# Copies of value sums and of transposed probabilities put ahead on ScalarE, the heads' norm as one power of a sum, three buffers zeroed by ScalarE

## The chip, the cores and the metric

The kernel runs on one core of a Trainium2 chip. The metric is the device time of one execution in microseconds (us), lower is better. Three runs of the kernel before took 1310.02, 1311.20 and 1311.35 us; the median is 1311.2 us. One more execution was taken with the hardware profiler on, and everything that is read from a trace below comes from it.

## The reference, cut to what matters

One step of a decoder layer with 512 prompt tokens and 32 sample tokens (8 sequences of 4), model width 1024. Three mixers work side by side (two convolutions and a 4-head mLSTM), then follow a cross attention over 256 memory tokens and a SwiGLU. The parts that the change touches are the keys and values of the memory, the norm of the mLSTM heads, and the softmax of the cross attention:

```
def memory_kv(mem, g, w_kv):
    kv = rmsnorm(mem, g) @ w_kv
    k, v = jnp.split(kv, 2, axis=-1)
...
        h = num / jnp.maximum(jnp.abs(den), floor)[..., None]
...
    hc = hc * lax.rsqrt(jnp.mean(hc * hc, axis=-1, keepdims=True) + EPS)
...
    pr = jax.nn.softmax(s, axis=-1).astype(h.dtype)
    out = jnp.einsum('bhtm,bmhd->bthd', pr, mv.astype(h.dtype)).reshape(B, T, HX * DX)
```

The sample tokens bring their own memory (32 key blocks and 32 value blocks of 256 KB, streamed from HBM) and their own mLSTM state.

## The kernel before, in words

**Tiling.** Activations stand transposed: channels on the 128 partitions, the 544 tokens along the free axis. Each float32 operand is split into a high and a low float32r part: ScalarE copies the high part, VectorE subtracts it from the source for the low part (`split`, lines 112 to 118). A product is three passes, high with high, high with low, low with high. Each 128-wide output block (`block`, line 291) has 48 matmuls of 272 columns. Its weights come as one 512 KB load into a raw buffer `wr` (4 of them) and are split into a buffer `w` (3 of them).

**Order.** TensorE's instructions run in the order in which the program emits them. Small steps are woven into a block through lists of tokens (`first_o`, `head_1`, `heads`, `after_heads` from line 922, `xside` and `xoside` from line 1341). For the other engines a planner chooses the order ahead of time: among the instructions that are ready by its own count it takes the one with the lowest number. The number is the place in the program, less 150 inside `evacuate`, less 300 for weight loads and their splits, less 600 inside `urgent`. Once planned, each engine, and each DMA queue, works through its list in that order; the head of a list that waits holds up all that is behind it.

**Memory values.** `mem_v` (line 526) multiplies the memory with a quarter of the value weights, in two halves; after the second half two sums [128, 256] stand in two of the four PSUM buffers `s1`. Two copies (line 539) scale them by `rm` and write them into `f1` buffers (ten in all), and from there go two DMAs each. In the first lists the order is: sum of squares for the memory norm (`C`, `mem_cols`), second half of quarter 0, first half of quarter 1, `R` (`mem_rows`: two transposes into another `s1` buffer), second half of quarter 1, the first key block, `t` (`token_cols`), and so on. At the same time ScalarE and VectorE work out the gates of the mLSTM (lines 621 to 670). Counted through the program, the first two copies of `mem_v` have the numbers 584 and 599, the ScalarE instructions of lines 655 to 670 the numbers 451 to 461.

**Heads' norm.** `finish` (line 886) adds the sample part of a head's numerator, squares it on ScalarE with a sum, takes the denominator and the norm through eight small [128, 5] instructions (seven on VectorE, one power on GpSimd), and scales the numerator by the result in five instructions (line 904). `head_out` (line 906) transposes it. For heads 0 to 2 this is emitted inside `evacuate`, for the last inside `urgent`.

**Cross attention.** Three buffers [128, 2, 576] (`mqx` and two of `pm`) are set to zero by GpSimd (lines 1190 to 1194); only their diagonal blocks are written later. `xs_t` (token `T`) transposes a half of the probabilities into one PSUM buffer and splits its two halves; `xs_pv` (token `V`) multiplies them with the values; `t` does the same for the sample tokens; `xs_kv` (token `K`) loads the keys and values of the next head back from HBM and splits them. In the list of block 3 stands `... a07 T01 T00 K1`, in that of block 4 `t0 - V0 ...`. The tokens `t` and `o` are emitted inside `evacuate`.

Of the kernel before, what the change touches and what calls it, by code (L numbers as in the profile page):

```python
# [11 lines left out]
AF = mybir.ActivationFunctionType  # L12
# [3 lines left out]
P = 128  # L16
D = 1024
NP = 512
NS = 32
# [5 lines left out]
NM = 256  # L25
EPS = 1e-6
# [9 lines left out]
def layer(ctx: ExitStack, tc: tile.TileContext, a):  # L36
    nc = tc.nc
# [23 lines left out]
    def pht(shape, dt=F32, tag=None, bufs=1):  # L61
        n = nm(tag or "ph")
        return ph["sb"].tile(shape, dt, tag=tag or n, name=n, bufs=bufs)
# [8 lines left out]
    def pair():  # L72
        return act_t([P, 2, T])

    def f1(shape=None, dt=F32):
        return sb.tile(shape or [P, T], dt, tag="f1", name=nm("f1"), bufs=10)

    def lt(shape=None, dt=F32):
        return sb.tile(shape or [P, T], dt, tag="lt", name=nm("lt"), bufs=8)

    def small(shape, dt=F32, tag="small", bufs=16, ZP=0):
        return (ph["sb"] if ZP else sb).tile(shape, dt, tag=tag, name=nm(tag), bufs=bufs)

    def const(shape, dt=F32):
        n = nm("const")
        return sb.tile(shape, dt, tag=n, name=n, bufs=1)
# [4 lines left out]
    def s1(shape):  # L91
        return ph["ps"].tile(shape, F32, tag="s1", name=nm("s1"), bufs=ph["s1"])

    def TTo(out, x, y, op):
        nc.vector.tensor_tensor(out=out, in0=x, in1=y, op=op)  # L95

    def TS(out, x, s1_, op0, s2=None, op1=None):
        if op1 is None:
            nc.vector.tensor_scalar(out=out, in0=x, scalar1=s1_, scalar2=None, op0=op0)
        else:  # L100
            nc.vector.tensor_scalar(out=out, in0=x, scalar1=s1_, scalar2=s2, op0=op0, op1=op1)

    def STT(out, x, s, y, op0, op1):
        nc.vector.scalar_tensor_tensor(out=out, in0=x, scalar=s, in1=y, op0=op0, op1=op1)  # L104

    def ACT(out, x, f, **kw):
        nc.scalar.activation(out, x, f, **kw)  # L107

    def MM(out, l, r, start, stop):
        nc.tensor.matmul(out, lhsT=l, rhs=r, start=start, stop=stop)  # L110
# [9 lines left out]
    def MS(ap, v):  # L120
        nc.gpsimd.memset(ap.bitcast(F32) if ap.dtype == F32R else ap, v)

    MULT, ADD, SUB, MAX, MIN = ALU.mult, ALU.add, ALU.subtract, ALU.max, ALU.min
# [11 lines left out]
    ones32 = const([P, P])  # L135
# [10 lines left out]
    for h in range(NH):  # L146
        for base in (20, 28, 36, 44):
            for d in range(2):
                order += [("in", base + 2 * h + d)]
                if base == 44 and h == 0 or h == 1 and base < 36:  # L150
                    n = (1, 7)[d] if h == 0 else 2
# [114 lines left out]
    def wget(*key):  # L266
        i = order.index(key)
        assert i == wpos[0] or key in wt, (key, order[wpos[0]])
        while wpos[0] <= min(i + ahead[0], len(order) - 1):
            w_emit(order[wpos[0]])  # L270
            wpos[0] += 1
        return wt.pop(key)
# [18 lines left out]
    def block(key, acts, nbg=0, inner=()):  # L291

        w = wget(*key)
        ps = mm_ps()
        nk, done = len(acts), 0
        for k in range(nk):
            mm_k(ps, w, acts, k, k == 0, k == nk - 1)
            while done < len(inner) and (done + 1) * nk <= (k + 1) * len(inner):
                if inner[done]:
                    inner[done]()  # L300
                done += 1
        background(nbg)
        return ps

    def evacuate(f):

        with tc.high_priority(EVAC):
            f()
# [175 lines left out]
    def part(f, *x):  # L484
        return lambda: f(*x)
# [4 lines left out]
    memg, mst = [], {}  # L490
# [32 lines left out]
    def mem_k(k, hl):  # L523
        return memg[k // 2][:, hl, k % 2, :]

    def mem_v(g, half):

        w = wget("v", g, half)
        if half == 0:
            mst["ps"] = [s1([P, NM]) for _ in range(2)]  # L530
        for mb in range(2):
            ps = mst["ps"][mb]
            for k in range(4 * half, 4 * half + 4):
                for n, (wi, ai) in enumerate(PASSES):
                    MM(ps, mem_k(k, ai)[:, mb * P:(mb + 1) * P], w[:, wi, (k % 4) * NM:(k % 4 + 1) * NM],
                       k == 0 and n == 0, k == 7 and n == 2)
            if half:
                vo = f1([P, NM])
                ACT(vo, ps, AF.Copy, scale=mst["rm"][:, mb:mb + 1])
                nc.sync.dma_start(out=a["pv"][:, mb, g * NM:(g + 1) * NM], in_=vo)  # L540
                nc.sync.dma_start(out=vscr[:, mb, g * NM:(g + 1) * NM], in_=vo)

# [70 lines left out]
    for k in range(8):  # L613
        STT(xr[k], xr[k], col(V_MIX, k), rx, MULT, MULT)
        p = pair()
# [229 lines left out]
    def numer(h, j):  # L845

        if j == 0:
            num = st[h]["num"] = pht([P, 5, E1], tag="num")
            ssq = st[h]["ssq"] = pht([P, 5], tag="ssq", bufs=2)
            MS(num[:, 4, :], 1.0)  # L850
            MS(ssq, 1.0)
        num, ssq, sp, vt = (st[h][x] for x in ("num", "ssq", "sp", "vt"))
        np_ = s1([P, E1])
        for i in range(j + 1):
            for x, (vi, si) in enumerate(PASSES):
                MM(np_, sp[i][:, si, (j - i) * P:(j - i + 1) * P], vt[i][:, vi, :], i == 0 and x == 0,
                   i == j and x == 2)
        ACT(num[:, j, :], np_, AF.Copy)
        ACT(np_[:, :NM], np_[:, :NM], AF.Square, accum_out=ssq[:, j:j + 1])

    def sample(h, b):

# [23 lines left out]
    def finish(h):  # L886

        num, ssq, nps = (st[h][x] for x in ("num", "ssq", "nps"))
        n2 = pht([NS, E1], tag="n2")
        ACT(n2, nps[32:64, :], AF.Copy)  # L890
        TTo(num[:NS, 4, :], nps[0:32, :], n2, ADD)
        ACT(n2[:, :NM], num[:NS, 4, :NM], AF.Square, accum_out=ssq[:NS, 4:5])
        dd, xx, rs = small([P, 5]), small([P, 5]), small([P, 5])
        STT(dd, num[:, :, NM], -1.0, num[:, :, NM], MULT, MAX)
        TTo(dd, dd, tcol[:, :, 64 + h], MAX)
        nc.vector.reciprocal(dd, dd)
        TTo(xx, ssq, dd, MULT)
        TTo(xx, xx, dd, MULT)
        TS(xx, xx, 1.0 / NM, MULT, EPS, ADD)
        nc.gpsimd.tensor_tensor(out=rs, in0=xx, in1=nhalf, op=ALU.pow)  # L900
        TTo(rs, rs, dd, MULT)
        for j in range(5):
            n = P if j < 4 else NS
            TS(num[:n, j, :NM], num[:n, j, :NM], rs[:n, j:j + 1], MULT)

    def head_out(h, d):
# [47 lines left out]
        7: "- - - o0 - o1",  # L954
    }
    before_ops = {"n": numer, "p": sample, "k": k_tok, "c": c_state, "o": head_out}
    head_ops = {"B": m_bcast, "S": scores, "s": scores_s, "V": v_tok}
    other_ops = {"I": mem_in, "t": token_cols, "C": lambda: urgent(mem_cols), "R": lambda: urgent(mem_rows)}

    def side(h, toks):  # L960
        r = []
        for t in toks.split():
            k, x = t[0], [int(y) for y in t[1:]]
            if k == "-":
                r.append(None)
            elif k == "M":
                r += mem_next(1)
            elif k == "P":
                r.append(part(sample, h, 0))
            elif k == "f":  # L970
                r.append(lambda: (urgent if h == NH else evacuate)(lambda: finish(h - 1)))
            elif k in before_ops:
                r.append(part(before_ops[k], h - 1, *x))
            elif k in head_ops:
                r.append(part(head_ops[k], h, *x))
            else:
                r.append(other_ops[k])
        return r
# [80 lines left out]
    for j in range(8):  # L1059
        p = pair()  # L1060
# [6 lines left out]
    for c in range(4):  # L1067
# [23 lines left out]
        p = pair()  # L1091
# [73 lines left out]
    for k in range(8):  # L1165
        x = lt()
# [21 lines left out]


    mqx = pht([P, 2, 576], F32R)  # L1190
    MS(mqx, 0.0)
    pm = [pht([P, 2, 576], F32R) for _ in range(2)]
    for x in pm:
        MS(x, 0.0)
    at = [None] * 8
    xs = [dict() for _ in range(4)]

# [164 lines left out]

    def xrun(t):
        f = part(xops[t[0]], *map(int, t[1:]))
        return (lambda: evacuate(f)) if t[0] in "to" else f

    def xlist(x):
        return [None if t == "-" else xrun(t) for t in x.split()]
# [5 lines left out]
    for j in range(2, 8):  # L1374

        ps = block(("xq", j), xg, inner=xlist(xside[j]))
# [7 lines left out]
    for j in range(8):  # L1384

        ps = block(("xo", j, 0), at[0:4], inner=xlist(xoside[j]))
# [342 lines left out]
```

## Time and profile before

| | |
|---|---|
| median of the runs shown | 1311.2 us (1310.02 to 1311.35) |
| the profiled execution's own time | 1310.46 us |
| its span, first to last instruction | 1308.5 us |
| TensorE matmuls busy | 1287.4 us, 98% |
| VectorE busy | 887.1 us, 68% |
| ScalarE busy | 592.8 us, 45% |
| GpSimd busy | 41.6 us, 3% |
| mean granted TensorE clock | 0.996 of full speed |

The profile gives for each instruction its start and length, and for each idle stretch the instruction whose semaphore ended it. Positions are microseconds from the first instruction. Instructions of one kind that follow each other on an engine are drawn together in a timeline line; "x4" is then their number and the length is that of all together. "L110" is the line of the helper that issues a matmul, L107 that of every ScalarE activation, L95 a VectorE operation on two tensors, L104 one with a scalar and two tensors, L99 and L101 one with scalars only, L121 a GpSimd fill. Between "[" and "]" stands how long the engine was idle before, and what it waited for.

### The profile page before, as it was taken

What the parts mean: (1) busy time and instruction counts of PE and PEld (TensorE: products, weight loads), DVE (VectorE), ACT (ScalarE), POOL (GpSimd) and SP (SyncE); (2) the same over time, 40 slices, a digit from 0 to 9 for tenths busy, and PEclk for the clock granted to TensorE, in tenths of its full rate; (3) what the DMA queues carried; (4) which work ended last, traced back from release to release, by engine and by line L of the source; (5) the groups of instructions that cost most, each with busy time, mean ns of one, the idle gap of its engine ahead of it and who ended that gap; (6) DMA issues with size and microseconds to landing.
All of it is one profiled execution on the core that took longest, in us unless ns stands there. A gap on an engine that the chain in (4) does not pass through costs nothing.

```text
span 1308.5 us, 24803 instructions
## 1 busy us (share of the span) xinstructions
PE 1287.4 (98%) x10164; PEld 1271.9 (97%) x10164; DVE 887.1 (68%) x1486; ACT 592.8 (45%) x1046; POOL 41.6 (3%) x117
## 2 busy tenths in 40 slices
PE   9989999999999999999999999999999999999997
PEld 9989999999999999999999999999999999999997
DVE  6965665655497859976434557886787667777746
ACT  6845545554433222226333446765544444444433
POOL 1000010110010000000000000000000000000000
PEclk9999999999999999999999999999999999999998
DMA  7365644434465233423244224664323233333212
GB/s 262 101 179 172 193 132 137 126 109 148 117 148 168 84 95 82 82 73 89 84 129 147 82 89 144 210 193 142 94 74 113 86 94 109 94 94 94 80 41 69
DMA packets 83265, 155.68 MB, mean 119 GB/s; under 512 B 25124, under 2 KB 33700, under 8 KB 83152
## 3 DMA queue, kind: packets, MB, share of 16 engines
q1 hardware_dynamic: 83152, 154.10, 40.1%
q8 instruction: 80, 1.31, 0.4%
q14 instruction: 33, 0.27, 0.1%
HBM read 137.54 MB, written 16.52 MB: 118 GB/s over the span
## 4 chain that ended last, share of the span: by engine, by line
PE 90%; issue 5%; DVE 2%; ACT 1%; DMA 1%; POOL 0%; SPq 0%; POOLq 0%; DVEq 0%; ACTq 0%
PE mm L110 62%; PE s L110 14%; PE sy L1477 8%; PE sz L1477 4%; PE sx L1477 2%; DVE f L95 0%; ACT w L107 0%; DVE w L95 0%; DMA f<-kscr 0%; ACT act L107 0%; PE s L911 0%; POOL small L381 0%; PE s L827 0%; DMA lt<-in_xT 0%; ACT f L107 0%
## 5 line engine op out<-in xcount | busy, mean ns | idle before, releaser
L110 PE MATMUL mm<-act,w 128*128 128x272 f32 x6336 | 838.0, 289 | 1.9 <-ACT f L107 0.9
L110 PEld LDWEIGHTS mm<-act,w 128*128 128x128 f32 x6336 | 809.7, 189 | 5.1 <-ACT f L107 1.1
L107 ACT ACTIVATE w<-wr 128x1024 fp32r<-128x1024 f32 (+2 forms) x202 | 196.6, 975 | 393.9 <-PE mm L110 229.2
L95 DVE TENSOR_TENSOR w<-wr,w 128x1024 fp32r<-128x1024 f32 (+2 forms) x202 | 225.4, 1116 | 142.7 <-ACT w L107 142.0
L104 DVE SCALAR_TENSOR_TENSOR f<-act,const,f 128x512 f32<-128x512 f32 (+1 forms) x136 | 96.4, 718 | 2.4
L95 DVE TENSOR_TENSOR lt<-mm,lt 128x544 f32<-128x544 f32 x56 | 40.4, 721 | 55.8 <-PE mm L110 55.6
L110 PE MATMUL mm<-act,fw 128*128 128x272 f32 x576 | 76.2, 288 | 0.0
L110 PEld LDWEIGHTS mm<-act,fw 128*128 128x128 f32 x576 | 73.9, 188 | 0.0
L107 ACT ACTIVATE act<-f 128x544 fp32r<-128x544 f32 (+3 forms) x75 | 44.3, 600 | 46.2 <-DVE f L95 40.8
L110 PE MATMUL s<-act,act 128*128 128x256 f32 (+4 forms) x408 | 62.9, 302 | 1.1 <-DVE act L95 0.8
L95 DVE TENSOR_TENSOR act<-f,act 128x544 fp32r<-128x544 f32 (+3 forms) x75 | 48.4, 652 | 20.6 <-ACT act L107 20.3
L95 DVE TENSOR_TENSOR f<-f,f 128x544 f32<-128x544 f32 (+4 forms) x78 | 51.2, 659 | 14.0 <-ACT f L107 12.7
L110 PEld LDWEIGHTS s<-act,act 128*128 128x128 f32 (+1 forms) x408 | 55.0, 184 | 4.2 <-DVE act L95 1.2
L1477 PE MATMUL sy<-bt,w 128*128 128x272 f32 x408 | 56.9, 288 | 0.6 <-ACT f L107 0.6
L1477 PEld LDWEIGHTS sy<-bt,w 128*128 128x128 f32 x408 | 53.3, 188 | 0.8 <-ACT f L107 0.8
L104 DVE SCALAR_TENSOR_TENSOR ct<-ct,wbc,s 128x258 f32<-128x258 f32 x64 | 28.7, 478 | 26.4 <-PE s L110 26.4
L107 ACT ACTIVATE f<-sy 128x272 f32<-128x272 f32 x51 | 19.7, 389 | 39.2 <-PE sy L1477 39.0
L95 DVE TENSOR_TENSOR wr<-wr,wr 128x1024 f32<-128x1024 f32 (+1 forms) x34 | 32.4, 954 | 5.9 <-DMA wr<-in_w_fi 5.5
L95 DVE TENSOR_TENSOR f<-mm,f 128x544 f32<-128x544 f32 (+1 forms) x29 | 20.7, 720 | 22.6 <-PE mm L110 20.4
L107 ACT ACTIVATE fw<-fr 128x512 fp32r<-128x512 f32 x26 | 16.4, 632 | 42.9 <-PE mm L110 41.6
L107 ACT ACTIVATE f<-mm 128x544 f32<-128x544 f32 (+1 forms) x50 | 30.5, 611 | 6.1 <-PE mm L110 5.9
L95 DVE TENSOR_TENSOR xpair<-kr,xpair 128x512 fp32r<-128x512 f32 x46 | 30.5, 681 | 3.5 <-ACT xpair L107 3.4
(237 smaller groups left out, 1405.5 us busy)
## 6 DMA issues: line engine op xcount, KB each, us to landing
wr<-in_w_in SPq DMA_DIRECT2D x74, 512.0 KB, 3.7
wr<-in_w_fi SPq DMA_DIRECT2D x44, 512.0 KB, 3.6
ct<-in_ctn SPq DMA_DIRECT2D x32, 258.0 KB, 3.0
out_sct<-ct SPq DMA_DIRECT2D x32, 258.0 KB, 3.3
kr<-in_ktc SPq DMA_DIRECT2D x32, 256.0 KB, 3.8
kr<-in_vc SPq DMA_DIRECT2D x32, 256.0 KB, 3.9
fr<-in_w_ffn_out SPq DMA_DIRECT2D x32, 256.0 KB, 2.7
lt<-in_xT SPq DMA_DIRECT2D x16, 272.0 KB, 3.7
```

What stands on the lines that cost most here:

```text
L95: nc.vector.tensor_tensor(out=out, in0=x, in1=y, op=op)
L104: nc.vector.scalar_tensor_tensor(out=out, in0=x, scalar=s, in1=y, op0=op0, op1=op1)
L107: nc.scalar.activation(out, x, f, **kw)
L110: nc.tensor.matmul(out, lhsT=l, rhs=r, start=start, stop=stop)
L1477: nc.tensor.matmul(ps, lhsT=w[:, wi, c + k * P:c + (k + 1) * P], rhs=x(k, ai), start=first and k == 0 and n == 0, stop=k == 3 and n == 2, ...
```

## The change

The copies of the value sums in `mem_v` go inside `evacuate`, and so do the steps of token `T`. The squares of the numerator are scaled by 1/16 before they are squared, so that the sum is the mean over 256. With d the greater of |den| and the floor, `finish` no longer divides: the factor (mean(num²)/d² + eps)^(-1/2) / d is written as (mean(num²) + eps·d²)^(-1/2). Three buffers are zeroed by ScalarE copies with the scale 0 in place of GpSimd fills.

```
             if half:
                 vo = f1([P, NM])
-                ACT(vo, ps, AF.Copy, scale=mst["rm"][:, mb:mb + 1])
+                evacuate(lambda: ACT(vo, ps, AF.Copy, scale=mst["rm"][:, mb:mb + 1]))
...
-        ACT(np_[:, :NM], np_[:, :NM], AF.Square, accum_out=ssq[:, j:j + 1])
+        ACT(np_[:, :NM], np_[:, :NM], AF.Square, scale=1.0 / 16, accum_out=ssq[:, j:j + 1])
...
-        ACT(n2[:, :NM], num[:NS, 4, :NM], AF.Square, accum_out=ssq[:NS, 4:5])
+        ACT(n2[:, :NM], num[:NS, 4, :NM], AF.Square, scale=1.0 / 16, accum_out=ssq[:NS, 4:5])
+
         dd, xx, rs = small([P, 5]), small([P, 5]), small([P, 5])
         STT(dd, num[:, :, NM], -1.0, num[:, :, NM], MULT, MAX)
         TTo(dd, dd, tcol[:, :, 64 + h], MAX)
-        nc.vector.reciprocal(dd, dd)
-        TTo(xx, ssq, dd, MULT)
-        TTo(xx, xx, dd, MULT)
-        TS(xx, xx, 1.0 / NM, MULT, EPS, ADD)
+        STT(xx, dd, EPS, dd, MULT, MULT)
+        STT(xx, xx, 1e-37, ssq, MAX, ADD)
         nc.gpsimd.tensor_tensor(out=rs, in0=xx, in1=nhalf, op=ALU.pow)
-        TTo(rs, rs, dd, MULT)
...
     mqx = pht([P, 2, 576], F32R)
-    MS(mqx, 0.0)
     pm = [pht([P, 2, 576], F32R) for _ in range(2)]
-    for x in pm:
-        MS(x, 0.0)
+    for x in (mqx, *pm):
+        ACT(x.rearrange("p a (n c) -> p (a n) c", c=64), ones32[:, 0:64].rearrange("p (o c) -> p o c", o=1)
+            .to_broadcast([P, 18, 64]), AF.Copy, scale=0.0)
...
     def xrun(t):
         f = part(xops[t[0]], *map(int, t[1:]))
-        return (lambda: evacuate(f)) if t[0] in "to" else f
+        return (lambda: evacuate(f)) if t[0] in "toT" else f
```

## Rows read from the trace of the kernel before

**Rows 1.** The first page of the profile: the busy times, with their share of the span, and the shares of the engines in the chain of work that ended last.

```profile
PE 1287.4 (98%) x10164; PEld 1271.9 (97%) x10164; DVE 887.1 (68%) x1486; ACT 592.8 (45%) x1046; POOL 41.6 (3%) x117
PE 90%; issue 5%; DVE 2%; ACT 1%; DMA 1%; POOL 0%; SPq 0%; POOLq 0%; DVEq 0%; ACTq 0%
```

**Rows 2.** The waits of TensorE over the whole span: who waited for whom, us in total, how often, the longest. The two longest are shown.

```profile
PE s L388 <- ACT f L107: 4.7, 1, 4.7
PE s L911 <- DVE num L99: 1.6, 1, 1.6
```

**Rows 3.** The timeline of TensorE from 64 to 84 us: start, length, line, operation.

```profile
64.67 5.92 PE L110 MATMUL s<-w,act 128*128 128x256 f32 x48
70.42 0.91 PE L110 MATMUL mm<-act,w 128*128 128x272 f32 x6
76.02 0.43 PE L388 MATMUL s<-const,const 128*128 128x128 f32 x2 [4.69 <-ACT f L107]
76.21 4.60 PE L110 MATMUL s<-w,act 128*128 128x256 f32 x24
80.65 3.04 PE L110 MATMUL s<-act,w 128*128 128x256 f32 x24
```

**Rows 4.** Busy times by stretch: start and end, length, busy us (instructions) of TensorE, weight loads, VectorE, ScalarE, GpSimd, then the granted TensorE clock, the busy share of the DMA engines and GB/s.

```profile
76.50:79.90 3.40, 3.40 (x18) 3.40 (x17) 0.00 (x0) 0.85 (x2) 0.00 (x0) 0.50 0.80 174
396.20:399.60 3.40, 3.40 (x27) 3.19 (x27) 1.51 (x2) 0.50 (x1) 0.00 (x0) 1.00 0.67 197
```

**Rows 5.** The timeline of ScalarE from 67 to 77 us. "f<-s,const" are the copies of the value sums, "w<-wr" high parts of weights, the rest the gates and, last, the copy of `mem_rows`.

```profile
67.75 1.06 ACT L107 ACTIVATE w<-wr 128x1024 fp32r<-128x1024 f32 x1 [2.23 <-PE s L110]
70.74 0.66 ACT L107 ACTIVATE ph<-f 4x544 fp32r<-4x544 f32 x1 [1.93 <-DVE f L648]
71.47 1.28 ACT L107 ACT_TABLE_LOAD   x1
72.76 0.65 ACT L107 ACTIVATE f<-f 4x544 f32<-4x544 f32 x1
73.44 1.06 ACT L107 ACTIVATE w<-wr 128x1024 fp32r<-128x1024 f32 x1
75.52 0.45 ACT L107 ACTIVATE f<-s,const 128x256 f32<-128x256 f32 x1
76.00 0.45 ACT L107 ACTIVATE f<-s,const 128x256 f32<-128x256 f32 x1
```

**Rows 6.** The timeline of VectorE in the same stretch: the copy of `rm`, the second scan of the gates, and the low parts of two weights.

```profile
66.43 0.49 DVE L515 COPY const<-small 128x2 f32<-128x2 f32 x1 [0.60 <-POOL small L381]
69.36 1.28 DVE L648 TENSOR_TENSOR_SCAN f<-f,f 4x544 f32<-4x544 f32 x1
71.32 1.21 DVE L95 TENSOR_TENSOR w<-wr,w 128x1024 fp32r<-128x1024 f32 x1
74.53 1.23 DVE L95 TENSOR_TENSOR w<-wr,w 128x1024 fp32r<-128x1024 f32 x1 [0.83 <-ACT w L107]
```

**Rows 7.** The timeline of all engines from 383 to 399 us, the last head's `finish`, the fills of the three buffers, and the first transposes of that head.

```profile
386.77 0.40 ACT L107 ACTIVATE n<-num 32x256 f32<-32x256 f32 x1
387.51 0.18 DVE L896 RECIPROCAL small<-small 128x5 f32<-128x5 f32 x1
390.06 1.66 POOL L900 TENSOR_TENSOR small<-small,const 128x5 f32<-128x5 f32 x1 [13.70 <-DVE small L101]
391.68 3.05 POOL L121 MEMSET ph<- 128x1152 f32 x3
395.02 1.02 PE L911 MATMUL s<-const,num 128*128 128x128 f32 x4 [1.64 <-DVE num L99]
397.77 0.60 PE L911 MATMUL s<-const,num 128*128 128x128 f32 x4
```

**Rows 8.** The five scalings of the numerator (L99), as a group: ns shortest, median, longest. The first line is the group from 392 to 396 us (last head), the second that from 180 to 182 us (first head).

```profile
L99 DVE TENSOR_SCALAR num<-num,small x5: 335/342/2383, 392.5 to 395.6; 128x256 f32<-128x256 f32 x4, 32x256 f32<-32x256 f32 x1
L99 DVE TENSOR_SCALAR num<-num,small x5: 336/350/354, 180.6 to 181.7; 128x256 f32<-128x256 f32 x4, 32x256 f32<-32x256 f32 x1
```

**Rows 9.** The timeline of ScalarE after the last head: the weight split at 411 us, and the idle time before it.

```profile
411.08 1.06 ACT L107 ACTIVATE w<-wr 128x1024 fp32r<-128x1024 f32 x1 [3.55 <-issue]
```

**Rows 10.** The timeline around the first `V` token. "act<-s" are parts of the transposed probabilities, "act<-f" the split of the next head's keys, L99 and L1300 the end of the sample's softmax and its transposes (`t0`).

```profile
795.22 0.34 DVE L99 TENSOR_SCALAR f<-f,small 32x256 f32<-32x256 f32 x1
795.49 0.74 DVE L95 TENSOR_TENSOR act<-s,act 128x256 fp32r<-128x256 f32 x2
796.05 0.31 PE L1300 MATMUL s<-const,f 32*128 32x32 f32 x2
797.02 0.63 ACT L107 ACTIVATE act<-f 128x512 fp32r<-128x512 f32 x1 [1.49 <-DMA f<-kscr]
797.89 0.86 PE L110 MATMUL s<-act,act 128*128 128x512 f32 x3
798.58 0.37 ACT L107 ACTIVATE act<-s 128x256 fp32r<-128x256 f32 x1
799.01 0.50 PE L110 MATMUL s<-act,act 128*128 128x512 f32 x1 [0.25 <-ACT act L107]
800.35 2.12 PE L110 MATMUL s<-act,act 128*128 128x512 f32 x8 [0.84 <-DVE act L95]
```

**Rows 11.** DMA issues: KB each, median us from issue to landing.

```profile
vscr<-f SPq DMA_DIRECT2D x8, 128.0 KB, 3.2
```

## The prediction, on record before the changed kernel ran

> **What bounds the kernel now.** I read the first page, then the waits of TensorE, then the timeline around each long wait. On the page the reader sees TensorE busy for 1287.4 us, 98% of the span, and in the chain that ended last 90% TensorE [rows 1]: VectorE and ScalarE have room, so an instruction less on them is worth only what TensorE waits for it. The list of waits then tells where: one of 4.7 us on a ScalarE result and one of 1.6 us on the scaling of a head's numerator [rows 2]. With two short ones of 0.25 and 0.84 us at the first `V` token [rows 10] these lie at the four places that the change touches, so each part is worked out from its own place.
>
> **1. The copies of the value sums.** TensorE reaches `R` at 71.33 us (six matmuls from 70.42 take 0.91) and stands until 76.02: four PSUM buffers hold the two finished sums of quarter 0 and the two half sums of quarter 1, and `R` needs one of them back [rows 3]. The sums ended near 67.6 us (half of the 48 matmuls from 64.67), `rm` was there at 66.92 [rows 6], but the copies start at 75.52 and 76.00 [rows 5], and TensorE goes on 0.05 us after the first ends. In front of them stand gate instructions and a table load; ScalarE even idles 1.93 us before 70.74, so something else held the copies as well. I take it to be their f1 buffer: the second scan of the gates, 69.36 to 70.64, is what sets two of the ten free [rows 6]. From 584 and 599 the change makes 434 and 449, below the gates' 451 to 461. So the copies go right behind the weight split that ends at 68.81, or at worst when the scan is through: 70.64 plus 0.45 is 71.1, before TensorE needs the buffer. Nothing on ScalarE but the gates is behind them, and these move by at most 0.9 us.
>
> The wait costs more than itself. After it the granted clock was 0.50 of full speed, 1.2 GHz, from 76.5 to 79.9 [rows 4], and the next 24 matmuls took 4.60 us where the following 24 took 3.04 [rows 3]: 1.6 us more. After the idle 1.64 us before 395.02 the clock stayed at 1.00 [rows 4, 7]. The whole is 4.69 + 1.6 = 6.3 us.
>
> Late next are the weights. The second half of quarter 1 needs the low part that VectorE makes from 71.32 to 72.53 [rows 6]: TensorE, at that matmul by 71.85, waits 0.7 to 0.8 us. It is through near 75.4. The first key block needs the low part that was made from 74.53 to 75.76 after a high part at 73.44 [rows 5, 6]; with the copies ahead that is up to 0.9 us later, so up to 76.6 against 75.65: 0 to 0.95 us. I take 0.8 + 0.9: the gain is 6.3 - 1.7 = 4.6 us. Bounds: 6.3 if both parts come early, 0 if the copies stay where they are. The three later pairs of copies ended no wait in the list of TensorE, and are put at nothing; their cover is the run of matmuls after them, and without it each would cost its 0.45 us.
>
> **2. The fills and the last head.** TensorE is at the transposes at 393.38 and gets the first scaled part at 395.02 [rows 7]. That scaling took 2.383 us where the median is 0.34 [rows 8]: it began at 392.5 and ended as the three fills on GpSimd ended (391.68 + 3.05 = 394.73). The four after it took 0.34 each, the five of the first head, with no fill beside them, 0.35. With the fills off GpSimd it would end near 392.85, before TensorE asks. So the wait of 1.64 us goes with the fills alone, and the four transposes, spaced by the scalings (1.02 us against 0.60 for the next four [rows 7]), give 0.42 more: 2.05 us.
>
> The Trainium skill ("SBUF — State Buffer", Who interferes with whom) has VectorE and GpSimd share one pair of ports as an exclusive lock in VectorE's 2-port modes, which `tensor_scalar` can enter; the other fully blocks. By it the whole 2.04 us of the long scaling go when the fills go; without it that scaling might have waited for something that stays, and the part would be worth only what the shorter chain gives. The trace agrees with it: a scaling that lasts until the last fill ends.
>
> The shorter chain is then cover only. Between the square (ends 387.2) and the power (390.06) stood four small instructions, so 0.7 us for each with what lies between them; now one, so the power, which ended at 391.72, ends near 389.6, and the first scaling, with the 0.8 us that lay between the two, near 390.8 [rows 7, 8]: 2.6 us before TensorE. The factor 1/16 rides in an instruction that is there. The earlier heads' norms end no wait of TensorE either; nothing is taken for them.
>
> The zeros on ScalarE are not in the trace. From 1.06 us for 1024 columns and 0.66 for 544 [rows 5], 1152 columns make some 1.17 us, three 3.5 us (an estimate). Their place in the list is the planner's. If it is after the last head, the idle 3.55 us before 411.08 [rows 9] hides them. If all three come ahead of the last square, the first scaling moves from 390.8 to 394.3, and 0.9 us of the wait stay. A gain of their own I exclude, since TensorE waits for none. I take nothing, by the idle row; the end 0.9 stays in the range.
>
> **3. Transposed probabilities.** The last quarter of the first head's split starts at 798.58 on ScalarE. Ahead of it stands, besides others, the split of the next head's keys, which waits 1.49 us for its DMA. `V` stops twice, 0.25 and 0.84 us idle [rows 10]; its twelve matmuls, which at the pace of the last eight (2.12 us) take 3.2 us, last from 797.89 to 802.47: 1.4 us lost. Both halves of a transposed tile lie in one PSUM buffer, and the low part of the other half ends at 796.23: if the last high part has to wait for that, it starts at 796.3 and is still in time for 797.89, unless it is again behind the key split. Against it: the sample's softmax now stands behind such splits of 0.37 us, two of them 0.7 us; it ended at 795.56, and its transposes `t0` ran at 796.05, 0.5 us later [rows 10]: up to 0.3 us would be waited there, 0.5 with a low part ahead too. Ends: +1.4 and, if the key split stays ahead and `t0` is late, -0.5. I take 0.9, the one less the other, for all four heads, as the other three show no wait to win.
>
> **The sum.** 4.6 + 2.05 + 0.9 = 7.55 us. Against the profiled execution's 1310.46 us that is 1302.9; this lies 0.74 below the median of the runs shown, so I add half of that: 1303.3 us.
>
> **Rivals.**
> (a) The wait moves to the weights: ScalarE's list puts the key block's high part last, behind all the gates [rows 5]: these end at 75.52, less its own 1.06, plus the copies' 0.9; with 1.06 and VectorE's 1.23 the low part is done at 77.7, TensorE idles 2.0 us instead of 0.9 and falls to 1.2 GHz again (1.6 us). For it: the gates and a table load of 1.28 us stand in the same list. Against it: the weight has the lower number. Then part 1 gives 6.3 - 0.8 - 2.0 - 1.6 = 1.9, the sum is 4.85 and the time 1306.0.
> (b) The change doesn't do what it says: the copies are not ready in the planner's count until the gates are done, and stay. For it: ScalarE idled before 70.74 and they were not taken. Against it: the scan frees buffers in time, and 434 is below 451. Then parts 2 and 3 are left: 1310.46 - 2.95 = 1307.5, and with part 3 at nothing 1308.4 (1309.1 from the median).
> (c) Slower. The copies hold f1 buffers until two DMAs have landed, 3.2 us in the median for the second [rows 11]. If they take them from the gates, the scan waits for a write, then the weight part behind it on VectorE; TensorE waits at quarter 1 as long as it did at `R` (6.3, no gain), and the exponentials of `m_bcast`, four f1 buffers more, wait for the writes of the next pair: two landings and a fall of the clock, 2 x 3.2 + 1.6 = 8.0. Then 1310.46 + 8.0 - 2.95 = 1315.5. It decides from the point where that second wait is over 2.95 us. For it: ten buffers, all in use at the scan. Against it: the copies come ready late in the planner's order, when the gates hold theirs already.
>
> **How the numbers follow.** Forecast 0.62, (a) 0.14, (b) 0.16, (c) 0.08. All terms in full (6.3 + 2.05 + 1.4) give 1300.7; the forecast's own range is 1300.5 to 1305.5. To leave out no more than 2 in 10 the range goes up to (b), 1309.0. About 0.2%, 2.6 us, is what a measurement can tell: faster is below 1308.6. The forecast, (a) and over half of (b) are faster, 0.85; the rest of (b), and (c) where its second wait is short, the same, 0.09; slower 0.06.
>
> **What would show it.** The timeline after: the copies before 71.5 us, `R` without a wait, the clock at 1.00 between 71 and 80, waits under 1 us at the next 48 matmuls (part 1, and (a) if one is longer than 2 us); the last head's five scalings at 0.35 us and no wait at its transposes (part 2); the twelve matmuls of the first `V` without a gap, and whether `t0` waits (part 3). The prediction is wrong if the first copy still starts after 72 us, if a scaling is long without a fill, or if TensorE shows a wait of over 3 us that is not in the list before.

## The result and the profile after

The changed kernel took 1304.3 us in the median of three runs, the kernel before, run beside it, 1311.0 us. The ratio of the means is 0.9947 with a 95% interval of 0.9928 to 0.9967: 6.9 us faster, by the interval 4.3 to 9.4. (A fourth run of the changed kernel was disturbed and took 4426 us; all figures here leave it out.) The forecast was 1303.3 us and faster. The execution whose trace is read below took 1301.8 us, 8.6 us less than the profiled one of the kernel before.

The first page of the profile after, the lines that answer to [rows 1]:

```profile
PE 1284.5 (99%) x10164; PEld 1269.8 (98%) x10164; DVE 883.9 (68%) x1474; ACT 596.2 (46%) x1049; POOL 38.3 (3%) x114
PE 89%; issue 4%; DVE 3%; DMA 2%; ACT 1%; POOL 0%; POOLq 0%; DVEq 0%; ACTq 0%
```

The instruction counts show the norm and the fills: 12 fewer on VectorE (three for each of four heads), three more on ScalarE and three fewer on GpSimd (the fills). The share of TensorE hardly moves, so the waits have to tell where the time went. The waits of TensorE over the whole span, as in [rows 2]:

```profile
PE s L110 <- DVE f L95: 1.5, 1, 1.5
...
PE mm L110 <- DVE lt L104: 1.0, 1, 1.0
...
PE s L110 <- DVE w L95: 0.9, 2, 0.7
...
PE s L1298 <- DVE f L99: 0.2, 1, 0.2
```

The two waits at the top of [rows 2], 4.7 and 1.6 us, are gone; the longest left, 1.5 us, stands in both kernels, far from the change. The other three lines shown are new: the two weights of part 1 (0.9 together), the sample's transposes `t0` of part 3 (0.2), and one of 1.0 us that the prediction did not have, a matmul of a block of the output weights that waits for `lt`.

TensorE's 10164 matmuls stand in the same order in both traces, so the time can be followed by comparing the start of the same matmul (us). The last column is what the change had won up to there, with the 1.09 us that lie ahead of all its parts:

| matmul | before | after | shift so far |
|---|---|---|---|
| six matmuls ahead of `R` | 70.42 | 69.33 | -1.09 |
| `R` | 76.02 | 70.11 | -5.91 |
| last matmul ahead of the last head's transposes | 393.10 | 387.12 | -5.98 |
| first transposes | 395.02 | 387.24 | -7.78 |
| second transposes | 397.77 | 389.56 | -8.21 |
| the matmul that waits for `lt` after the change | 404.73 | 397.56 | -7.17 |
| `t0` of the first head | 796.05 | 789.17 | -6.88 |
| first matmul behind the first `V` | 802.30 | 793.75 | -8.55 |
| end of the span | 1308.5 | 1299.9 | -8.6 |

**Part 1.** The timeline of all engines from 65 to 76 us, against [rows 3, 5, 6] (start, length, engine, line, operation, and in brackets the idle time ahead of it and what ended it):

```profile
68.27 1.28 DVE L648 TENSOR_TENSOR_SCAN f<-f,f 4x544 f32<-4x544 f32 x1
...
69.33 0.91 PE L110 MATMUL mm<-act,w 128*128 128x272 f32 x6
...
69.58 0.84 ACT L107 ACTIVATE f<-s,const 128x256 f32<-128x256 f32 x2 [1.87 <-DVE f L648]
...
70.11 0.43 PE L388 MATMUL s<-const,const 128*128 128x128 f32 x2
70.22 1.21 DVE L95 TENSOR_TENSOR w<-wr,w 128x1024 fp32r<-128x1024 f32 x1
...
71.48 2.89 PE L110 MATMUL s<-w,act 128*128 128x256 f32 x22 [0.70 <-DVE w L95]
...
72.41 1.06 ACT L107 ACTIVATE w<-wr 128x1024 fp32r<-128x1024 f32 x1
...
73.50 1.23 DVE L95 TENSOR_TENSOR w<-wr,w 128x1024 fp32r<-128x1024 f32 x1 [1.74 <-ACT w L107]
...
74.63 0.66 ACT L107 ACTIVATE ph<-f 4x544 fp32r<-4x544 f32 x1
...
74.78 1.93 PE L110 MATMUL s<-act,w 128*128 128x256 f32 x14 [0.17 <-DVE w L95]
```

The copies start at 69.58, in the moment at which the second scan of the gates ends (68.27 + 1.28 = 69.55): nothing but the f1 buffer ties a copy to that scan, so it was the buffer that they had to wait for. `R` follows its six matmuls without a wait. Then come the two weights, 0.70 and 0.17 us. The clock in the same stretch of time as in the first of [rows 4], and over the work behind `R`:

```profile
76.50:79.90 3.40, 3.40 (x32) 3.40 (x32) 2.65 (x3) 1.75 (x3) 0.00 (x0) 1.00 0.78 256
71.50:80.00 8.50, 8.33 (x69) 8.13 (x70) 5.07 (x11) 6.66 (x13) 0.00 (x0) 1.00 0.85 234
```

It is 1.00 throughout: 2.4 GHz where [rows 4] has 0.50. The 22 matmuls behind the weight wait take 2.89 us, where the 24 of that half took 4.60 in [rows 3].

**Part 2.** The last head's scalings as a group, as in [rows 8], and the timeline around them and the next block:

```profile
L99 DVE TENSOR_SCALAR num<-num,small x5: 336/347/354, 383.3 to 384.4; 128x256 f32<-128x256 f32 x4, 32x256 f32<-32x256 f32 x1
```

```profile
381.64 1.67 POOL L899 TENSOR_TENSOR small<-small,const 128x5 f32<-128x5 f32 x1 [11.27 <-DVE small L104]
...
387.24 0.60 PE L909 MATMUL s<-const,num 128*128 128x128 f32 x4
...
391.26 0.63 ACT L107 ACTIVATE k<-kr 128x512 fp32r<-128x512 f32 x1 [6.77 <-DMA kr<-in_ktc]
391.92 0.69 DVE L95 TENSOR_TENSOR k<-kr,k 128x512 fp32r<-128x512 f32 x1 [3.94 <-ACT k L107]
...
393.20 0.90 DVE L104 SCALAR_TENSOR_TENSOR lt<-s,const,lt 128x512 f32<-128x512 f32 x2
...
395.65 2.20 ACT L107 ACTIVATE ph<-const 128x1152 fp32r<-128x1152 f32 x2
...
397.17 0.24 DVE L104 SCALAR_TENSOR_TENSOR lt<-s,const,lt 128x32 f32<-128x32 f32 x1
...
397.56 2.62 PE L110 MATMUL mm<-act,w 128*128 128x272 f32 x19 [0.99 <-DVE lt L104]
```

No scaling is long, and they begin at 383.3, 3.9 us before TensorE asks. Then something is given back. The evacuations of the transposed head, `lt`, stand on VectorE behind the low part of a streamed key block `k`, and that behind the key block's high part, which waited 6.77 us for its DMA. The zeros of ScalarE (1.10 us each) stand behind that, and hold up nothing on TensorE.

**Part 3.** The timeline around the first `V`, against [rows 10]:

```profile
788.77 0.34 DVE L99 TENSOR_SCALAR f<-f,small 32x256 f32<-32x256 f32 x1
789.17 0.31 PE L1298 MATMUL s<-const,f 32*128 32x32 f32 x2 [0.24 <-DVE f L99]
...
789.41 0.36 ACT L107 ACTIVATE act<-s 128x256 fp32r<-128x256 f32 x1
...
790.00 1.33 ACT L107 ACTIVATE act<-f 128x512 fp32r<-128x512 f32 x2 [0.16 <-DMA f<-kscr]
...
791.01 2.90 PE L110 MATMUL s<-act,act 128*128 128x512 f32 x12
```

The last quarter of the split ("act<-s" at 789.41) now stands ahead of the key split ("act<-f"), and the twelve matmuls of `V` run in 2.90 us without a gap. `t0` waits 0.24 us for the sample's softmax.

### The profile page after: what moved, and what is told of

Read it like the earlier page. It is cut to its first block, busy times and chain, and to the rows that moved or that the text cites. A ratio compares the mean times of both kernels' runs of the same rounds, so it can differ in the third digit from the quotient of the medians.

```text
span 1299.9 us, 24786 instructions
## 1 busy us (share of the span) xinstructions
PE 1284.5 (99%) x10164; PEld 1269.8 (98%) x10164; DVE 883.9 (68%) x1474; ACT 596.2 (46%) x1049; POOL 38.3 (3%) x114
## 4 chain that ended last, share of the span: by engine, by line
PE 89%; issue 4%; DVE 3%; DMA 2%; ACT 1%; POOL 0%; POOLq 0%; DVEq 0%; ACTq 0%
PE mm L110 61%; PE s L110 14%; PE sy L1475 8%; PE sz L1475 4%; PE sx L1475 2%; DMA out_sct<-ct 1%; DVE f L95 1%; DVE w L95 0%; DMA kr<-in_vc 0%; DMA kr<-in_ktc 0%; DVE xpair L95 0%; ACT w L107 0%; ACT f L107 0%; ACT act L107 0%; DVE f L104 0%
```

## Experiments

Eleven kernels were run, in three groups, each group on one chip beside its own runs of the kernel before (medians 1309.35, 1310.27 and 1309.8 us, 29, 12 and 21 runs). 0.001 of a ratio is 1.3 us. Ratios are to the kernel before.

**The four parts, each alone on the kernel before.** The edits are those hunks of the diff, one by one: the copies; the fills; the squares and `finish`; the token `T`.

> The kernel before with the copies of the value sums inside evacuate, and nothing else. Theory (the wait at R and the fall of the clock after it are one cost): the first copy starts when the second scan of the gates ends, R has no wait, the granted clock stays at 1.00, the next 48 matmuls wait 0.7 and 0.2 us for weight parts; 4.9 us shorter up to the end of the first key block, and the whole 4.9 us shorter, ratio 0.996. Rival (the clock falls there for a reason of its own): the clock still goes to 0.50 for some 3.4 us, and only 3.4 us are won, ratio 0.9974.

> The kernel before with the three buffers zeroed by ScalarE, and nothing else. Theory (GpSimd's fills hold up VectorE's scaling): the first scaling of the last head takes 0.35 us instead of 2.38, the transposes have no wait, 2.1 us are won there, and 1.0 is given back at the next output block, where TensorE waits for the head's product with its gate; the whole 1.1 us shorter, ratio 0.9992. Rival (that scaling waited for something else that ended with the fills): it stays above 2 us and nothing is won, ratio 1.000.

> The kernel before with the heads' norm as one power of a sum (squares scaled by 1/16), and nothing else. Theory (either edit alone removes the wait): the power ends 2.1 us earlier, the fills follow it and still hold the first scaling to over 2 us, but that now ends some 0.7 us before TensorE asks; the same 2.1 us are won and 1.0 given back, ratio 0.9992. Rival (the fills set the time whatever the chain does): TensorE still waits over 1 us at the transposes, ratio 1.000.

> The kernel before with token T inside evacuate, and nothing else. Theory (the last high part was late behind the split of the next head's keys): the twelve matmuls of the first V run without a gap, 1.5 us won, t0 waits 0.2 to 0.3; the whole 1.2 us shorter, ratio 0.9991. Rival (the gain needs the earlier edits, since the planner's order shifts with them): the key split stays ahead, V waits as before, ratio 1.000 to 1.0003.

| part alone | median us | ratio, interval |
|---|---|---|
| copies | 1303.5 | 0.9956 (0.9944 to 0.9968) |
| fills | 1309.0 | 0.9999 (0.9989 to 1.0008) |
| norm | 1308.9 | 0.9997 (0.9988 to 1.0005) |
| `T` | 1308.9 | 0.9993 (0.9985 to 1.0002) |

The copies alone bring 5.8 us (4.2 to 7.3). In their trace `R` has no wait, and the clock does not fall:

```profile
71.60:80.00 8.40, 7.82 (x65) 7.62 (x66) 4.97 (x11) 7.09 (x13) 0.00 (x0) 1.00 0.79 235
```

That is part 1 by itself, with the same two weight waits (0.9 us together), so rivals (a) and (b) are out. The other three parts, each alone, cannot be told from nothing by the times. In its trace each takes its wait away; the norm and `T` find another, the fills do not. With the fills off GpSimd no scaling is long (ns shortest, median, longest):

```profile
L99 DVE TENSOR_SCALAR num<-num,small x5: 335/348/349, 391.0 to 392.1; 128x256 f32<-128x256 f32 x4, 32x256 f32<-32x256 f32 x1
```

There is no wait at the transposes, and none for `lt` either: the 1.0 us that was expected to be given back is not, in this execution. That the times of eleven runs still show only 0.1 us (-1.0 to 1.4) fits a wait that is mostly shorter in the kernel before than the 1.64 us of the one execution, as is seen below. With the shorter norm the fills still hold the first scaling:

```profile
L99 DVE TENSOR_SCALAR num<-num,small x5: 335/342/3132, 388.6 to 392.4; 128x256 f32<-128x256 f32 x4, 32x256 f32<-32x256 f32 x1
```

The power ends 3.2 us earlier than in [rows 7]: 0.7 of this is the whole execution standing earlier there, 0.9 an earlier split of the key block that stands ahead of the last square on ScalarE, and some 1.6 the shorter chain. So the scaling, though held for 3.13 us, is through before TensorE asks at 392.53 (393.38 before): no wait at the transposes here either. 0.4 us are then waited for `lt` at the next block, 0.63 and 0.83 us at the first `V` (0.25 and 0.84 in [rows 10]), and 0.7 us at a later `t0`. And with `T` alone the first `V` has no gap:

```profile
794.30 0.31 PE L1300 MATMUL s<-const,f 32*128 32x32 f32 x2 [0.23 <-DVE f L99]
...
796.14 2.90 PE L110 MATMUL s<-act,act 128*128 128x512 f32 x12
```

What these single parts showed besides is that the wait at the last head's transposes is not fixed. With the norm and the fills as before it was 1.6 us in [rows 2], and 0.6 with the copies alone and 0.7 with `T` alone. What is fixed is its distance from the power: in all three traces the transposes start 3.31 us after the power ends, which is the 3.05 us of the fills and 0.26 more. The power itself moves with the key block's split ahead of the last square.

**The fills doubled, on the kernel before.**

```diff
     for x in pm:
         MS(x, 0.0)
+    for x in (mqx, *pm):
+        MS(x, 0.0)
```

> The kernel before with each of the three buffers filled twice by GpSimd (the second fill writes the same zeros). Theory (a scaling that meets a fill is held until GpSimd's fills are through): the first scaling ends as the sixth fill ends, 3.05 us later than before, so it takes 5.4 us, TensorE waits 3.7 to 4.7 us at the transposes, and the kernel is 3 us slower, more if the clock falls after that wait; ratio 1.0024 or above. Rival (the scaling waits for something else): it still takes 2.4 us, ratio 1.000.

1314.6 us, ratio 1.0029 (1.0019 to 1.0039). The group of the scalings, the transposes and the clock by stretch (columns as in [rows 4]):

```profile
L99 DVE TENSOR_SCALAR num<-num,small x5: 334/341/5383, 392.6 to 398.7; 128x256 f32<-128x256 f32 x4, 32x256 f32<-32x256 f32 x1
```

```profile
391.79 6.05 POOL L121 MEMSET ph<- 128x1152 f32 x6
```

```profile
398.14 1.17 PE L911 MATMUL s<-const,num 128*128 128x128 f32 x4 [4.46 <-DVE num L99]
...
399.48 3.09 PE L110 MATMUL mm<-act,w 128*128 128x272 f32 x12
```

```profile
400.00:403.00 3.00, 3.00 (x16) 3.00 (x14) 3.00 (x7) 0.72 (x2) 0.00 (x0) 0.50 0.59 155
403.00:406.00 3.00, 3.00 (x19) 2.60 (x19) 3.00 (x6) 3.00 (x6) 0.00 (x0) 0.76 0.61 153
```

Three more fills make the one scaling 3.00 us longer (5.38 for 2.38), by as much as the fills grew (6.05 for 3.05), and the wait grows by 2.8. The transposes start 6.30 us after the power ends, for 3.31 before. Behind the wait of 4.46 us the clock is at 0.50, and stays there until 404.4 us: twelve matmuls take 3.09 us where they take 1.78 in both kernels, and up to 404.2 the same matmuls fall another 2.3 us behind those of the kernel before. Both together make 5.1 us in this pair of executions, of which this one, 1315.9 us, is among the two slowest of its eight runs; the ratio says 3.8 (2.5 to 5.1). The fills do hold the scaling.

**The changed kernel again, and with GpSimd's fills put back.**

```diff
     mqx = pht([P, 2, 576], F32R)
+    MS(mqx, 0.0)
     pm = [pht([P, 2, 576], F32R) for _ in range(2)]
-    for x in (mqx, *pm):
-        ACT(...)
+    for x in pm:
+        MS(x, 0.0)
```

> The changed kernel once more, beside the three below on one chip. Theory (the four terms as the traces have them, the last head's term smaller than in the one profiled execution because the load of a key block lands earlier in most): the copies 5.0, token T 1.0 to 1.2, the last head 0 to 1; 6 to 7 us shorter than before, ratio 0.9947 to 0.9954. Rival (the terms of the first trace hold on average): 7.4 us, ratio 0.9943.

> The changed kernel with the three buffers filled by GpSimd again. Theory (with the shorter chain the fills are early enough): the first scaling takes about 3 us but ends before TensorE asks, no wait at the transposes, the time of the changed kernel within 0.5 us, ratio 0.995. Rival (moving the fills is what gave the last head's term): a wait of 0.5 us or more is back at the transposes, and the ratio is 0.0005 to 0.0015 higher than that of the changed kernel.

The changed kernel: 1303.2 us, 0.9938 (0.9926 to 0.9951), with the same waits in its trace (0.7 us at `lt`). That is below what either side of its expectation had (0.9943 and more), though the interval reaches both. With the fills back: 1302.4 us, 0.9936 (0.9922 to 0.9951), no wait at the transposes, and 0.2 us at `lt`. Its first scaling is held again, for 3.13 us, and that costs nothing: it starts at 384.5 and TensorE asks at 388.53. So beside the shorter norm, moving the fills adds nothing that these times can show.

**The key blocks' place in the lists.** The wait for `lt` and the varying wait at the transposes both pointed at two streamed key blocks, whose split has buffers of its own and so can stand far ahead in the lists. In this edit the first ones use the common buffers, and their split moves behind the last head's products:

```diff
-        if n % 7 in (2, 5):
+        if n % 7 in (2, 5) and n > 6:
```

> The changed kernel with the first two prefetched key blocks that went to the buffers shared with the mLSTM state put into the cross attention's own buffers, so that their splits stand behind the last head's products in both lists. Theory (the wait of 1.0 us after the last head is a key block's load at the head of ScalarE's and VectorE's lists): no wait for the head's product at the next output block, 0.5 to 1.3 us shorter than the changed kernel, ratio to before 0.994 to 0.9945. Rival (the product is late for its own reasons): that wait stays, or the key blocks come too late at the start of the cross attention, and the time is that of the changed kernel or longer.

> The kernel before with one edit: the first two key blocks of the stream that would be split into their own pair of buffers use the common ones, so that their splits stand behind the last head's products in the lists. Fills, norm and copies are as before. Theory (the wait at the last head's transposes was so long in the profiled execution because a key block's split stood ahead of the last square on ScalarE and waited for its transfer): the idle time of 2.6 us ahead of the square's list goes, and the wait at the transposes, 1.6 us before and 0.6 to 0.7 in other executions, falls below 0.3 us with the scaling still held by the fills; the time is 0.6 to 1.6 us shorter (ratio 0.9988 to 0.9995). Rival (the held scaling alone makes the wait): 0.6 to 1.6 us stay at the transposes and the ratio is 1.000.

> The changed kernel with both edits that took waits away at the last head: GpSimd fills the buffers again, and the first key blocks use the common buffers. Theory (the two waits that the last head has in the changed kernel are gone, nothing else moves): neither a wait at the transposes nor one at the next block, 0.3 to 1.0 us below the changed kernel, ratio 0.992 to 0.9945 to the kernel before. Rival (the fills hold the scaling again and, with the split out of the way, it shows): a wait of 0.3 us or more at the transposes and no gain over the changed kernel.

The other traces say how the wait for `lt` hangs on the second of these splits. In six traces that have this split TensorE does not wait at the transposes: the fills alone, the changed kernel with the fills back, the norm alone, the changed kernel again, the changed kernel, and the changed kernel without the copies (below). There ScalarE starts the split 3.02, 3.18, 3.40, 3.74, 4.02 and 5.36 us after the transposes, and the wait for `lt` is 0, 0.16, 0.38, 0.72, 0.99 and 2.34 us: what the split is later than 3.02 us, TensorE waits.

On the changed kernel: 1302.3 us, 0.9935 (0.9923 to 0.9948). The wait for `lt` is gone from its list, but `t0` waits 0.6 us instead, and the 0.8 us to the changed kernel beside it lie within the intervals. With the fills back as well: 1302.8 us, 0.9941 (0.9927 to 0.9954); neither wait at the last head is there, and 1.1 us are waited at two places of `t0`. The gain of 0.3 to 1.0 us that was expected of it does not show; it ran in another group than the changed kernel, so only the ratios compare. No version beats the changed kernel by what can be measured.

On the kernel before: 1307.6 us, 0.9984 (0.9975 to 0.9993), so 2.1 us faster, more than expected. Its trace agrees with the expectation only in part. ScalarE's list, where [rows 7] has the square at 386.77 behind a key split that sat idle for 2.62 us:

```profile
382.35 0.38 ACT L107 ACTIVATE n<-s 32x258 f32<-32x258 f32 x1
383.94 0.42 ACT L107 ACTIVATE n<-num 32x256 f32<-32x256 f32 x1 [1.21 <-DVE num L95]
```

The square comes 2.8 us earlier, but the power only 1.7 (388.35 for 390.06), and 0.9 of either is the whole execution standing earlier there: on VectorE one instruction of some 0.75 us still stands between every two of the small ones. At the transposes 0.8 us are left, not under 0.3 as the theory had it, and again 3.31 us after the power ends. Another part was won where this edit has nothing to do: at the first `V`, whose matmuls run without a gap in that trace though `T` stands as before, since the planner's order came out otherwise there too.

**The changed kernel without the copies.**

```diff
-                evacuate(lambda: ACT(vo, ps, AF.Copy, scale=mst["rm"][:, mb:mb + 1]))
+                ACT(vo, ps, AF.Copy, scale=mst["rm"][:, mb:mb + 1])
```

> The changed kernel with the copies of the value sums left to the planner's order as before. Theory (the copies carry nearly 5 us of the gain, the other parts a net 1 to 2.3 us): the wait of 4.7 us behind the value sums and the lower clock after it are back, the ratio to the kernel before is 0.998 to 0.9993. Rival (the parts only pay together, so that without the copies nothing is left): 0.9995 to 1.0005. A second rival (the other parts carry most of it): below 0.997.

1307.9 us, 0.9985 (0.9977 to 0.9994): 2.0 us (0.8 to 3.0) for the three other parts together, as the theory had it. With the copies' 5.8 that makes 7.8, against 8.1 (6.4 to 9.7) for the whole change in the group before. The waits of TensorE in its trace:

```profile
PE s L388 <- ACT f L107: 4.7, 1, 4.7
PE mm L110 <- DVE lt L104: 2.3, 1, 2.3
```

The wait at `R` is back, and here the wait for `lt` is 2.3 us: as much as the last head's transposes had won. ScalarE's key split had waited 8.11 us for its DMA in that execution.

## Why the prediction was right, and where its terms were off

**Part 1** was predicted at 4.6 and measured at 4.9 us in the trace (from -1.09 to -5.98 in the table), 5.8 by the times of the copies alone. Its mechanism held step for step: the f1 buffer freed by the second scan held the copies, they start 0.03 us after it, `R` has no wait, the weights are late next, and the clock does not fall. Two terms were off. The 1.6 us of clock were 1.4 (the shift grows from -5.05 to -6.44 over the matmuls that were slow before). And the wait at the first key block, taken as 0.9 in the range of 0 to 0.95, was 0.17 us in the list and 0.44 in the shift: its high part came at 72.41 and not 0.9 us later than before, since one gate step ("ph<-f", 0.66 us), which stood ahead of it at 70.74 in [rows 5], stands behind it at 74.63. The planner, not the program alone, orders that list. The first weight was right: 0.8 predicted, 0.70 us idle. Rival (a) needed a wait of 2 us at the first key block, rival (b) copies after 72 us; neither is in the trace. Rival (c) is out as well: the scans wait for no landing of a copy's DMA.

**Part 2** had the right mechanism and too large a term. In the pair of profiled executions it came much as forecast, 2.23 us (from -5.98 to -8.21) for 2.05. But the term was taken from one execution, in which ScalarE's list had stood 2.62 us for a key block that landed late; in two others with the same fills and norm the wait was 0.6 and 0.7 us. And half of it went back at the next block, 0.99 us (1.04 in the shift), where `lt` stands behind the second key block's split. The step that failed is "So the wait of 1.64 us goes with the fills alone", booked as a gain of that size: the wait went, but its size was that of one execution, and behind it stood a second one, which comes and goes with the landing of the second key block (0 to 2.34 us in the six traces above). By the times the part is worth 0.1 us with the fills alone (-1.0 to 1.4) and 0.4 with the norm alone (-0.7 to 1.6). What is late next had been asked for the weights and not here.

That the fills held the scaling is shown by doubling them. That the shorter chain "is then cover only" held, and more: it works the other way round too. Either of the two edits removes the wait at the transposes. The zeros on ScalarE cost nothing, as put: they stand behind the last head, with 1.10 to 1.15 us each (an estimate of 1.17 had been made).

**Part 3** was predicted at 0.9, the difference of 1.4 at `V` and 0.5 at `t0`. `V` won 1.67 us (from -6.88 to -8.55) and `t0` waits 0.24 us (0.29 in the shift), so some 1.4 in this pair. By the times it is 0.9 alone (-0.3 to 2.0), which cannot be told from nothing; that the part pays rests on the traces. `t0` waits less than the upper end since the exponential of the sample's softmax, not a low part, was what came later.

**The sum.** By the shifts 4.89 + 2.23 - 1.04 - 0.29 + 1.67 = 7.46 us lie in the parts, where the forecast had 7.55. That the sum is so close is luck: 0.3 us more in part 1, 0.2 at the transposes and 0.5 in part 3 make up for the 1.04 at `lt` that it did not have, and the wait of 1.64 us was longer in the one execution than in three others. The other 1.1 us of the 8.6 between the two profiled executions stand ahead of 12 us (see the last section) and are not the change's. In the medians of the first runs the change brought 6.7 us and in those of the second group 7.1.

## What to carry to other kernels

When two waits of the busiest engine follow each other closely, ask of the second what it hangs on before the first is booked as a gain: here an evacuation stood in an in-order list behind the split of a block whose DMA was on the way, and took back half. A wait read from one execution, in front of which another engine sat idle for a DMA, is a sample and not a constant; take its size from more than one trace, or put the other end into the range. And a wait behind which the clock falls costs more than itself (here 1.4 us more behind 4.69 and 2.3 more behind 4.46), so those are worth taking first.

## What the runs showed of the hardware

**Fills back to back do not let a scaling in between.** In [rows 7, 8] the first scaling began after the first of three fills had started and ended with the last; with six it lasted 5.38 us and again ended as the last one ended (392.6 + 5.4 = 398.0; 391.79 + 6.05 = 397.84). A single fill seems to hold a copy in the same way: the [128, 2] copy of `rm` in [rows 6] takes 0.49 us and ends at 66.92, and a fill beside it ends at 66.90. Not every VectorE instruction is held: one on three operands that lies between the start of the first fill and the scaling took its usual time.

```profile
66.36 0.54 POOL L121 MEMSET f<- 68x544 f32 x1
...
391.83 0.75 DVE L104 SCALAR_TENSOR_TENSOR f<-act,const,f 128x512 f32<-128x512 f32 x1
```

The Trainium skill ("SBUF — State Buffer", Who interferes with whom) says that whichever is issued first gets the shared ports for the whole instruction and that the other blocks. By that the scaling could have had its turn when the first fill, 1.06 us, was through. The traces agree with the blocking, as the prediction said, but not with its length: it lasts for the whole row of fills.

**The clock after a wait.** Behind idle 4.69 us (at `R`) and 4.46 us (doubled fills) TensorE ran at 0.50, 1.2 GHz, until 3.9 us after the one wait and 6.3 us after the other; behind 2.34 us (the changed kernel without the copies), 1.64, 0.99 and 0.70 it stayed at 1.00. The length of one wait is not all: at the end of both kernels, with few matmuls left, the clock falls to 0.50 at 1301.87 and 1292.95 us, and no idle stretch there is longer than 1.47 us.

**The first microseconds vary with the clock.** Busy times of TensorE from 10.5 to 11 us, before and then after (the number in brackets is that of the matmuls):

```profile
10.50:11.00 0.50, 0.50 (x4) 1.00 1.05 409
```

```profile
10.50:11.00 0.50, 0.50 (x6) 1.00 1.05 405
```

Both print a granted clock of 1.00, yet the same kind of matmul is slower in the one. The 1.00 is no reading there: the trace's record of the granted clock begins with a rise to 1.00, at 11.64 us before and at 9.54 us after, and the view prints 1.00 where there is no record. Ahead of that rise matmuls of 272 columns follow each other every 227 ns in both traces, behind it every 125 or so. In the doubled fills they follow each other every 227 ns as well while the clock is at 0.50, so TensorE ran at the lower level, 1.2 GHz, until the rise. Of the 1.09 us at the top of the table 0.48 are lost earlier, by an idle 0.45 us ahead of 7.29 that the execution after does not have; the rest is the later rise. In the other profiles of this study the record begins between 10.0 and 12.2 us, and TensorE was between 0.9 us earlier and 0.2 us later than in the kernel before, with parts of the change or without. Why the rise comes sooner in one execution than in another stays open.
